# One layer on one core: the opening's weights get two places back in the load queue, and the forget chain runs early on 128 partitions

## The chip, the core and the metric

The kernel runs on one core of one Trainium2 chip. The metric is the device time of one launch, in microseconds (us). Five engines work side by side, each through its own list of instructions in order: TensorE (PE, with weight loads as PEld), VectorE (DVE), ScalarE (ACT), GpSimd (POOL) and SyncE (SP). SP and POOL issue nearly all DMA transfers here; an instruction that waits for a semaphore holds what is behind it on its engine.

## The reference

A decoder layer in float32 for 512 tokens of width 2048: two groups of eight attention heads from one input projection, one output projection, RMSNorm before and after.

```python
h = _rms_norm(x, g_pre)
proj = h @ w_in                      # 2048 x 6472
(q_lat, kv_lat, k_rope_raw, gate_mla,
 fq, fk, fv, f_logit, gate_fox) = jnp.split(proj, split_points, axis=-1)
o_mla = _mla_branch(q_lat, kv_lat, k_rope_raw, ..., cos, sin) * silu(gate_mla)
o_fox = _fox_branch(fq, fk, fv, f_logit, b_forget) * silu(gate_fox)
x = x + _rms_norm(concat([o_mla, o_fox]) @ w_out, g_post)
# in _fox_branch, before its causal softmax attention:
log_f = log_sigmoid(f_logit + b_forget)          # 512 tokens x 8 heads
c = cumsum(log_f, axis=1)
logits = q @ k.T * scale + c[query] - c[key]
# in _mla_branch 64 dimensions of each query and key are turned by the angles
# positions * inv_freq (cos, sin)
```

## The kernel before

Every float32 product is made of three fp32r matmuls: each operand is split into a rounded high part and the rest. For weights, `divide(i)` does this to chunk i: ACT casts `raw` to `whi` (L282), DVE subtracts to get `wlo` (L283). A chunk is mostly 128 partitions x 1024 columns (512 KB); raw, whi and wlo have three buffers each in the pool `wp`. `chunk(i)` asks for the loads of the next chunks and for the splits of the next two. The three matmuls of a term stand at L149, L150 and L151; L150 uses the moving operand's low part or wlo, L151 the other.

The work, in the order of the program:

- *Opening* (`proj_first`). x comes in nine loads (L187, L178: `xa`). For each of 16 blocks k of 128 input columns TensorE transposes the four token tiles (L530), ACT and DVE make `h` (L141, L142), and twelve matmuls (L645) form 328 columns of `w_in`: 256 of the latent, 64 of the rotary key, 8 forget logits. Chunks 0 and 1 hold one block each, chunks 2 to 8 two each. ACT also squares x for the norm (L540). Here ACT, DVE and PE keep the order as written (`manual_schedule`).
- *fq*: chunks 9 to 12, the first pair of FoX queries.
- *v and g* (FoX values and gates): seven products of half size in place of eight, p1, p2, g5, g3, g7, q6, p4, each over four chunks for v and four for g. Chunks 13 to 20 are p1, 21 to 28 p2, 29 to 36 g5, and so on up to chunk 68. The raws of p1 are loaded by `fill` (L235) into tiles `rawv` and `rawg`, five of them in the pool `vr`. When such a chunk is split, POOL adds the next block onto its raw tile by an accumulating DMA (L237). The raws of p2 (L249) take slots of the pool `sp`, which has 28 slots of 4 KB per partition, shared with x, h and most other tiles.
- *Sums of h* for those products (`x_steps`, beside fq and p1): DVE forms `xr` (L1104) and their differences `rmg` (L1003), splits some (L139), and POOL sends each to DRAM (L993, `awaymg`); only when that has landed is its slot free. SP fetches them again later (L1032, `bmg`, `bmq`).
- *Forget chain*. `forget_parts` scales rotary key and logits by the norm's factor (`rft`, tokens on partitions, L781); `rows` transposes that to `rf` (L796, L797), heads on partitions 64 to 71. Then sixteen steps on 8 partitions x 512 columns (tiles `fz`, `fw`, `fd`) form log_sigmoid (L800 to L829) and a scan sums it (L817); SP writes it to `c_dram` (L818). All but `rows` follow the g3 products in the program.
- *Rotary tables*: positions are loaded (L863), 25 DVE steps reduce the angles (L870 to L905), ACT takes three sines (L904 to L907), POOL writes them to DRAM and SP reads them back into `sinT` and `cosT` (L913).
- Then FoX attention, the MLA latents, MLA attention and the output projection. Beside them sums of weight blocks for w_ukv (`t7u` and others) and w_out are made in DRAM, by SP's load and POOL's accumulating DMA (`add_step`, L321, L325).

Outside the opening a scheduler orders each engine's list by its own estimate of when operands are ready; SP's and POOL's transfers can so move far ahead of their place in the program. `in_order` pins an instruction behind the one traced before it on its engine.

Of the kernel before, what the change touches and what calls it, by code (L numbers as in the profile page):

```python
# [12 lines left out]
F32 = mybir.dt.float32  # L13
F32R = mybir.dt.float32r
I32 = mybir.dt.int32
AF = mybir.ActivationFunctionType
ALU = mybir.AluOpType
AX = mybir.AxisListType

P = 128  # L20
D = 2048
S = 512
NT = S // P
NK = D // P
HW = 128
NH = 8
NOPE, ROPE, DV = 128, 64, 128
# [6 lines left out]
O_KR = O_KV + KVR  # L34
# [4 lines left out]
O_F = O_FV + NH * HW  # L39
# [4 lines left out]
L4 = KVR // 2  # L44
KL = L4 + ROPE
# [20 lines left out]
def tile_hybrid_layer(  # L66
# [16 lines left out]
    nc = tc.nc  # L83
    pe, act, dve, pool = nc.tensor, nc.scalar, nc.vector, nc.gpsimd
# [14 lines left out]
    def slot(name, dt=F32, shape=(P, 2, S)):  # L99

        return sp.tile(list(shape), dt, tag="s", name=name)
# [20 lines left out]
    def whole_block(wholes, i, src, scale=None):  # L122
# [5 lines left out]
            act.mul(to, src[:, :P], scale)  # L128
        return to

    def in_order(*instructions):

        for i in instructions:
            tc.keep_in_program_order(i)
# [72 lines left out]
    def add_chunks(w, cols, nk, per, width, first_k=0, single=0):  # L207


        first = len(chunks)  # L210
        k = 0
        while k < nk:
            n = min(1 if k < single else per, nk - k)
            chunks.append((w, cols, first_k + k, n, width))
            k += n
        return range(first, len(chunks))
# [6 lines left out]
    def raw_tile(i):  # L223
        if i in up_chunks:
            return slot(f"raw{i}", shape=(P, 1024))
        pool = more[0] if more and (i - more[1]) % 6 < 3 else wp
        return pool.tile([P, 1024], F32, tag="raw", name=f"raw{i}", bufs=3)

    def fill(i, raw):

        raws[i] = raw
        to = raw.rearrange("p (k c) -> p k c", k=2)
        first, second = chunks[i][0]
        if first is not None:
            in_order(nc.sync.dma_start(to, first))  # L235
        if second is not None:
            pool.dma_start(to, second, accum_op=ALU.add)  # L237

    def load(i, small=None):

        w, cols, k, n, width = chunks[i]
        assert state["step"] >= needs.get(i, -3) + 2
        if cols == "chain":
            return
        if cols is None:

            raw = raw_tile(i)
            for a, b in alike(raw, w):
                nc.sync.dma_start(a, b)  # L249
            raws[i] = raw  # L250
            if k is not None:
                second = slot(f"second{i}")
                nc.sync.dma_start(second, k)
                raws[i] = raw, second.rearrange("p k c -> p (k c)")
            return
        if i < 2:
            raw = slot(f"raw{i}", shape=(P, 1024))
        else:
            raw = raw_tile(i)
        v = raw[:, : n * width].rearrange("p (k c) -> p k c", k=n)  # L260
        for at, off, cnt in cols:
            (nc.sync if cnt >= P or small is None else small).dma_start(
                v[:, :, at : at + cnt],
                w[0, k * P : (k + n) * P, off : off + cnt].rearrange("(k p) c -> p k c", p=P),
            )
        raws[i] = raw

    def join(i):
# [39 lines left out]
    def alike(to, w):  # L308

        if len(w.shape) == 4:  # L310
            to = to.rearrange("p (k h x) -> p k h x", k=2, h=4)
            return [(to[:, k], w[:, k]) for k in range(2)]
        return [(to if len(w.shape) == 2 else to.rearrange("p (k c) -> p k c", k=2), w)]

    def add_step(n, mark):


        if n > 0:
            to, _, second = bg[n - 1]
            for a, b in alike(to, second):  # L320
                pool.dma_start(a, b, accum_op=ALU.add)  # L321
        if 0 <= n < len(bg):
            to, first, _ = bg[n]
            for a, b in alike(to, first):
                nc.sync.dma_start(a, b)  # L325
        if n + 1 < len(bg):
            nc.sync.dma_start(bg[n + 1][0][0:1, 0:16], mark)

# [54 lines left out]
    def plain_in(g, h, c):  # L383
        add_chunks(w_in, [(0, AT[g] + 512 * c, 512)], 8, 2, 512, 8 * h)

    first = add_chunks(w_in, [(0, O_KR - L4, KL), (KL, O_F, NH)], NK, 2, KL + NH, single=2)
    fox = [{} for _ in range(4)]
    chain = {}

# [192 lines left out]
    def wait(n):  # L582
        todo.extend([lambda: None] * n)
# [177 lines left out]
        return g  # L761


    bcol = cst.tile([P, 1], F32, name="bcol")
    pool.memset(bcol, 0.0)
    nc.sync.dma_start(bcol[ROPE : ROPE + NH, :], b_forget.rearrange("o h -> h o"))
    rf = tb.tile([P, S], F32, name="rf")
    pool.memset(rf, 0.0)
    c_dram = dr.tile([NH, S], F32, name="c_dram")
# [2 lines left out]
    def forget_parts(o):  # L772

        r = tmp("rft")
        n = ROPE + NH
        for t in range(NT):
            c = slice(t * n, t * n + NH), slice(t * n + NH, (t + 1) * n)

            for a, b in ((c[0].start, L4), (c[0].start + ROPE, KL)):
                m = ROPE if b < KL else NH  # L780
                dve.tensor_scalar(  # L781
                    out=r[:, a : a + m], in0=o[t][:, b : b + m], scalar1=rcol[:, t : t + 1], scalar2=None,
                    op0=ALU.mult,
                )
        return r

    def forget_sums(r):

        zu, wl, dz = (slot(f"f{i}") for i in "zwd")
        z, u, w, ln, d, zrow = (a[R, i, :] for a in (zu, wl, dz) for i in range(2))  # L790
        n = ROPE + NH

        def rows():
            pt = att_bank("rf")
            for t in range(NT):
                pe.transpose(pt[:n, t * P : (t + 1) * P], r[:, t * n : (t + 1) * n], ident)  # L796
            dve.tensor_copy(rf[:n, :], pt[:n, :])  # L797

        def number(to, src, a, op, b=None, op2=None):
            return lambda: dve.tensor_scalar(  # L800
                out=to, in0=src, scalar1=a, scalar2=b, op0=op, **({"op1": op2} if op2 else {})
            )

        def two(to, x, y, op):
            return lambda: dve.tensor_tensor(out=to, in0=x, in1=y, op=op)

        def both(to, x, a, y, op0, op1):
            return lambda: dve.scalar_tensor_tensor(out=to, in0=x, scalar=a, in1=y, op0=op0, op1=op1)

        def logs():  # L810
            act.activation(ln, w, AF.Ln)

            act.activation(dummy, warm[:, 0:1], AF.Exp)

        def scan():
            pool.memset(zrow, 0.0)
            dve.tensor_tensor_scan(rf[R, :], z, zrow, 0.0, op0=ALU.add, op1=ALU.add)  # L817
            nc.sync.dma_start(c_dram, rf[R, :])  # L818

        return [  # L820
            rows,
            number(z, rf[R, :], bcol[R, :], ALU.add),
            both(u, z, -1.0, z, ALU.mult, ALU.min),
            lambda: act.activation(u, u, AF.Exp),
            number(w, u, 1.0, ALU.add),
            logs,
            number(w, w, -1.0, ALU.add),
            number(d, w, 1e-30, ALU.max),
            lambda: dve.reciprocal(d, d),  # L829
            two(ln, ln, d, ALU.mult),  # L830
            two(ln, ln, u, ALU.mult),
            number(d, w, 0.0, ALU.is_equal),
            two(d, d, u, ALU.mult),
            two(ln, ln, d, ALU.add),
            both(z, z, 0.0, ln, ALU.min, ALU.subtract),
            number(z, z, -1.0, ALU.mult),
            scan,
        ]

    def load_keys(h, wholes):  # L840
        both = slot(f"nk{h}")
# [14 lines left out]

    def rotary_tables():
        ifc = cst.tile([P, 2], F32, name="ifc")
        nc.sync.dma_start(ifc, inv_freq)
        rows = cst.tile([P, 3, P], F32, name="angles")  # L860
        r, n1, n2 = (rows[:, i, :] for i in range(3))
        for b in range(NT):
            nc.sync.dma_start(  # L863
                r[32 * b : 32 * (b + 1), :].bitcast(I32),
                positions[:, b * P : (b + 1) * P].to_broadcast([32, P]),
            )
        steps = []

        def angles():
# [371 lines left out]

    vb = [proj_bank(f"in{t}") for t in range(NT)]
    with tc.manual_schedule(engines={mybir.EngineType.Activation, mybir.EngineType.DVE, mybir.EngineType.PE}):
        proj_first(first, vb)
    make_rcol()
    rft = forget_parts(vb)
    l4 = slot("l4", shape=(P, NT, L4))
# [6 lines left out]
    wait(2)  # L1254
    todo.append(lambda: make_row(rrow, "rrow", *dg))
    set_pace(1000)
    todo.append(fs[0])
    todo.extend([*x_steps(0), *x_steps(1)])
    places = [(g, j) for g in "vg" for j in range(4)]
    for g, j in places[:5]:  # L1260
        fill(prods["p1", g][j], vr.tile([P, 1024], F32, tag="raw", name=f"raw{g}{j}", bufs=5))
# [94 lines left out]
    for g in "vg":  # L1356
# [4 lines left out]
    products(  # L1361
        "vg",
        {
            ("g5", "v"): (1, d3), ("g5", "g"): (1, f7), ("g3", "g", "after"): lambda: todo.extend([*fs[1:], *rotary_tables()]),
            ("g3", "v"): (1, d7), ("g3", "g"): (1, f6), ("g7", "v"): (1, d6),
        },
        out_of,
# [16 lines left out]
    for p in range(4):  # L1384
# [13 lines left out]
            vt = v_slot(3)  # L1398
            later = split_v(3, vt)
        if p == 2:  # L1400
            nc.sync.dma_start(gains[0:6, :], g_q.rearrange("o (k p) -> (o k) p", p=P))
            nc.sync.dma_start(gains[6:10, :], g_kv.rearrange("o (k p) -> (o k) p", p=P))
            make_gcol(gains, NK, 10)
        vs = values_of(f"fv{3 - p}")
        heads = []
# [502 lines left out]
```

## Time and profile before

| What | us |
|---|---|
| Median of 3 runs (lowest, highest) | 914.05 (913.49, 914.98) |
| Profiled execution, its own time | 913.19 |
| Span in its trace | 911.3 |
| PE busy, DVE busy, ACT busy | 881.8, 634.9, 500.7 |
| Mean granted clock | 0.989 |

Busy times are sums over an engine's instructions in the span. "Idle before" stands in brackets in a row, with what ended it. An SPq or POOLq row is the issue of a transfer, and its landing comes later. The rows of a view of stages give the stage's bounds and length, then for PE, PEld, DVE, ACT and POOL the busy time and the number of instructions.

### The profile page before, as it was taken

The page shows a single profiled execution, that of the slowest core. Times are in us where ns is not written, and L with a number is a line of the kernel's source. Part 1 is how long each engine was busy: PE and PEld are TensorE (multiplying, and loading weights), DVE is VectorE, ACT ScalarE, POOL GpSimd, SP SyncE. Part 2 cuts the span into 40 slices and gives each one's busy share as a digit, 9 for nine tenths or more (in the row PEclk, how much of TensorE's full clock was granted, in tenths as well). Part 3 has the DMA queues.
Part 4 walks back from the last instruction along what each step waited for, and adds up shares of the span by engine and source line. Part 5 has one row for each costly group of instructions (what it writes and reads, how often), then busy time and mean ns, then how long its engine had stood idle before and what let it go on. Part 6 is the DMA issues. An engine that isn't in the chain of part 4 may idle for free.

```text
span 911.3 us, 13774 instructions
## 1 busy us (share of the span) xinstructions
PE 881.8 (97%) x5078; PEld 775.2 (85%) x5078; DVE 634.9 (70%) x1056; ACT 500.7 (55%) x915; POOL 125.4 (14%) x133
## 2 busy tenths in 40 slices
PE   9699999989999999999999999999999999999996
PEld 8688899979988888888998999997888888887885
DVE  4589466598555455646655766899797895988786
ACT  6474454445336454444744444557766877645483
POOL 0114103433100010100022344100000000000021
PEclk9799999999999999999999999999999999999999
DMA  9859969989569889884699999568894235789878
GB/s 303 214 167 304 306 200 191 215 160 254 149 144 248 237 216 219 224 202 134 201 285 328 312 225 206 107 198 192 216 212 131 95 116 188 248 315 308 270 223 248
DMA packets 128360, 198.41 MB, mean 218 GB/s; under 512 B 16210, under 2 KB 61164, under 8 KB 127268
## 3 DMA queue, kind: packets, MB, share of 16 engines
q1 hardware_dynamic: 101300, 136.28, 47.8%
q0 software_dynamic: 26256, 61.02, 34.0%
q8 instruction: 40, 0.66, 0.3%
q10 hardware_dynamic: 736, 0.22, 0.1%
q14 instruction: 28, 0.23, 0.1%
HBM read 182.60 MB, written 44.25 MB: 249 GB/s over the span
## 4 chain that ended last, share of the span: by engine, by line
PE 85%; DMA 5%; DVE 5%; ACT 3%; issue 1%; SPq 1%; DVEq 0%; ACTq 0%
PE fq L149 3%; PE fk L151 3%; PE fk L149 3%; PE fk L150 3%; PE fq L151 3%; PE fq L150 3%; PE sm L688 3%; DMA raw<-in_w_in_dram 3%; PE mq L149 2%; PE mq L150 2%; PE mq L151 2%; PE oc L149 2%; PE oa L151 2%; PE oa L150 2%; PE oc L151 2%; PE oc L150 2%
## 5 line engine op out<-in xcount | busy, mean ns | idle before, releaser
L283 DVE TENSOR_TENSOR wlo<-raw,whi 128x1024 fp32r<-128x1024 f32 (+3 forms) x159 | 186.5, 1176 | 117.9 <-ACT whi L282 115.8
L282 ACT CAST whi<-raw 128x1024 fp32r<-128x1024 f32 (+3 forms) x159 | 160.6, 1012 | 160.2 <-PE fk L150 35.4
L149 PE MATMUL fk<-h,whi 128*128 128x512 f32 x128 | 52.5, 410 | 0.0
L149 PE MATMUL fq<-h,whi 128*128 128x512 f32 x128 | 51.0, 399 | 0.0
L151 PE MATMUL fk<-h,wlo 128*128 128x512 f32 x128 | 50.3, 393 | 0.0
L150 PE MATMUL fk<-h,whi 128*128 128x512 f32 x128 | 50.0, 391 | 0.0
L151 PE MATMUL fq<-h,wlo 128*128 128x512 f32 x128 | 50.0, 391 | 0.0
L150 PE MATMUL fq<-h,whi 128*128 128x512 f32 x128 | 50.0, 390 | 0.0
L282 ACT CAST whi<-rawg 128x1024 fp32r<-128x1024 f32 x24 | 25.2, 1051 | 36.2 <-PE vc L151 13.6
L282 ACT CAST whi<-rawv 128x1024 fp32r<-128x1024 f32 x24 | 25.2, 1050 | 34.0 <-PE gg L150 9.2
L282 ACT CAST whi<-rawl 128x1024 fp32r<-128x1024 f32 x25 | 26.2, 1048 | 31.1 <-PE mc L150 7.5
L283 DVE TENSOR_TENSOR wlo<-rawl,whi 128x1024 fp32r<-128x1024 f32 x25 | 30.5, 1223 | 18.0 <-ACT whi L282 18.0
L283 DVE TENSOR_TENSOR wlo<-rawv,whi 128x1024 fp32r<-128x1024 f32 x24 | 29.3, 1223 | 18.1 <-ACT whi L282 18.0
L283 DVE TENSOR_TENSOR wlo<-rawg,whi 128x1024 fp32r<-128x1024 f32 x24 | 29.2, 1222 | 11.2 <-ACT whi L282 11.2
L706 ACT ACTIVATE pf<-pf,stf 128x128 f32<-128x128 f32 (+3 forms) x32 | 18.0, 563 | 31.0 <-DVE stf L697 30.9
L1728 POOL DMA_DIRECT2D c<-in_x_dram x8 | 7.0, 1012 | 202.6 <-ACT c L1727 202.6
L645 PE MATMUL in<-whi,h 128*128 128x328 f32 x128 | 31.4, 333 | 3.4 <-ACT whi L282 3.4
L237 POOL DMA_DIRECT2D rawl<-in_w_in_dram x20 | 23.8, 1192 | 53.5 <-PE ptf L715 31.2
L149 PE MATMUL mq<-ln,whi 128*128 128x512 f32 x72 | 29.0, 403 | 0.0
L151 PEld LDWEIGHTS fq<-h,wlo 128*128 128x128 f32 x128 | 24.0, 188 | 5.3
L151 PEld LDWEIGHTS fk<-h,wlo 128*128 128x128 f32 x128 | 24.0, 188 | 5.3
L151 PE MATMUL mq<-ln,wlo 128*128 128x512 f32 x72 | 28.4, 394 | 0.0
(633 smaller groups left out, 2938.1 us busy)
## 6 DMA issues: line engine op xcount, KB each, us to landing
raw<-in_w_in_dram SPq DMA_DIRECT2D x62, 512.0 KB
raw<-in_w_out_dram SPq DMA_DIRECT2D x32, 512.0 KB
rawl<-in_w_in_dram POOLq DMA_DIRECT2D x20, 512.0 KB, 12.6
rawv<-in_w_in_dram POOLq DMA_DIRECT2D x16, 512.0 KB, 7.2
rawg<-in_w_in_dram POOLq DMA_DIRECT2D x16, 512.0 KB, 9.5
raw<-in_w_in_dram POOLq DMA_DIRECT2D x12, 512.0 KB, 11.9
bmg<-awaymg SPq DMA_DIRECT2D x20, 256.0 KB
rawl<-in_w_in_dram SPq DMA_DIRECT2D x10, 512.0 KB
```

Source lines behind the costliest of these rows:

```text
L149: pe.matmul(o, ah, bh, start=first, stop=False, **kw)
L150: pe.matmul(o, ah, bl, start=False, stop=False, **kw)
L151: pe.matmul(o, al, bh, start=False, stop=last, **kw)
L237: pool.dma_start(to, second, accum_op=ALU.add)
L282: act.copy(hi[:, :m], raw[:, :m])
L283: dve.tensor_tensor(out=lo[:, :m], in0=raw[:, :m], in1=hi[:, :m].bitcast(F32), op=ALU.subtract)
L645: pe.matmul(banks[t][:, :n], a[k][:, tss[t]], b[:, j, :], start=k == 0 and m == 0, stop=k == NK - 1 and m == 2,)
L688: pe.matmul(s[:, :nn], a[:, qs], c[:, :nn], start=(i == 0), stop=(i == len(pairs) - 1))
L706: act.activation(p, p, AF.Exp, bias=st[:, 0:1], scale=unit, accum_out=st[:, 1:2])
L1728: pool.dma_start(to, x[piece(t, c)], accum_op=ALU.add)
```

## The change

There are four parts.

1. *Two places.* `raw_tile` gives chunks 5 and 6 of the opening a tile of the pool `vr`, so they need no buffer that an earlier chunk has to leave.
2. *Nothing ahead.* `queued()` puts SP's transfers behind the load that `load` issued last (`tc.issue_after`: order of issue alone, no wait). It is used for first blocks of `fill`, the sums' loads in `add_step`, the bias, positions and the gains.
3. *Forget chain.* The bias joins in the scaling (one operation on 8 columns per token tile, as many as before). Twelve steps then run on 128 partitions x 32 columns in place, in three groups; `rows` and the scan follow. All of it is put in the program beside fq, and the rotary tables keep their place after g3.
4. Three tiles of 8 x 512 become one (`fz`, zeroed by POOL at the start).

```diff
+    def queued():
+        return tc.issue_after(state["last"])
...
     def raw_tile(i):
+        if i <= opening[-1] and i % 5 < 2:
+            return vr.tile([P, 1024], F32, tag="raw", name=f"raw{i}", bufs=5)
...
         if first is not None:
-            in_order(nc.sync.dma_start(to, first))
+            with queued():
+                nc.sync.dma_start(to, first)
...
+            if small is None:
+                state["last"] = last.ins
...
-    bcol = cst.tile([P, 1], F32, name="bcol")
-    pool.memset(bcol, 0.0)
-    nc.sync.dma_start(bcol[ROPE : ROPE + NH, :], b_forget.rearrange("o h -> h o"))
+    bias = cst.tile([P, NH], F32, name="bias")
+    with queued():
+        nc.sync.dma_start(bias, b_forget.to_broadcast([P, NH]))
...
+            dve.scalar_tensor_tensor(
+                out=r[:, a + ROPE : a + n], in0=o[t][:, KL : KL + NH], scalar=col, in1=bias,
+                op0=ALU.mult, op1=ALU.add,
+            )
...
-        z, u, w, ln, d, zrow = (a[R, i, :] for a in (zu, wl, dz) for i in range(2))
+        z = r[:, : NT * n].rearrange("p (t n) -> p t n", n=n)[:, :, ROPE:]
+        u, w, ln, d = (
+            r[:, NT * n + few * i : NT * n + few * (i + 1)].rearrange("p (t h) -> p t h", h=NH) for i in range(4)
+        )
...
+        return [powers, logs, ends, rows, scan]
...
-    todo.append(fs[0])
-    todo.extend([*x_steps(0), *x_steps(1)])
+    todo.extend(fs[:3])
+    wait(1)
+    todo.extend([*fs[3:], *x_steps(0), *x_steps(1)])
...
-            ... ("g3", "g", "after"): lambda: todo.extend([*fs[1:], *rotary_tables()]),
+            ... ("g3", "g", "after"): lambda: todo.extend(rotary_tables()),
```

The order that comes of it, at three places. In these rows a tile's name is followed by its number in the program (the first chunk's raw is raw0, then a serial number); lines are those of each version's own file, and the new version's stand 6 to 14 further down. First SP's list from the fourth piece of x on, before and then with the change:

```order
L178 DMA xa4_150<-in_x_dram 128x4x256
L178 DMA xa5_155<-in_x_dram 128x4x256
L178 DMA xa6_160<-in_x_dram 128x4x256
L178 DMA xa7_162<-in_x_dram 128x4x256
L766 DMA bcol_167<-in_b_forget_dram 8x1
L235 DMA rawv0_670<-in_w_in_dram 128x2x512
L235 DMA rawv1_672<-in_w_in_dram 128x2x512
L235 DMA rawv2_674<-in_w_in_dram 128x2x512
L235 DMA rawv3_676<-in_w_in_dram 128x2x512
L262 DMA raw5_152<-in_w_in_dram 128x2x320
```

```order
L181 DMA xa4_150<-in_x_dram 128x4x256
L268 DMA raw5_152<-in_w_in_dram 128x2x320
L268 DMA raw5_152<-in_w_in_dram 128x2x8
L181 DMA xa5_155<-in_x_dram 128x4x256
L268 DMA raw6_157<-in_w_in_dram 128x2x320
L268 DMA raw6_157<-in_w_in_dram 128x2x8
L181 DMA xa6_160<-in_x_dram 128x4x256
L181 DMA xa7_162<-in_x_dram 128x4x256
L775 DMA bias_167<-in_b_forget_dram 128x8
L268 DMA raw7_329<-in_w_in_dram 128x2x320
```

Chunks 5 and 6 move between the last pieces of x; chunks 7 to 12 follow, then the fills rawv0 to rawg3, the positions, c_dram and the raws of p2. The new raw12 waits, as before, for the split of raw9 to leave its buffer.

Next DVE's list among the splits of q6's chunks (wlo54 and wlo55 belong to v), before and then with the change; gc and vc are results of g and v.

```order
L283 TENSOR_TENSOR wlo54_1910<-rawv1_672,whi54_1909 128x1024
L829 RECIPROCAL fd_669<-fd_669 8x512
L139 TENSOR_TENSOR bmq63_1713<-bmq63_1713 128x512
L805 TENSOR_TENSOR fw_668<-fw_668,fd_669 8x512
L1296 TENSOR_TENSOR gc2_1508<-gc2_1508,gc0_1814 128x2x256
L805 TENSOR_TENSOR fw_668<-fw_668,fz_667 8x512
L800 TENSOR_SCALAR fd_669<-fw_668 8x512
L1296 TENSOR_TENSOR gc3_1509<-gc3_1509,gc1_1815 128x2x256
L805 TENSOR_TENSOR fd_669<-fd_669,fz_667 8x512
L283 TENSOR_TENSOR wlo55_1945<-rawv2_674,whi55_1944 128x1024
```

```order
L291 TENSOR_TENSOR wlo53_1896<-rawv0_666,whi53_1895 128x1024
L291 TENSOR_TENSOR wlo54_1927<-rawv1_668,whi54_1926 128x1024
L1309 TENSOR_TENSOR gc2_1523<-gc2_1523,gc0_1831 128x2x256
L1309 TENSOR_TENSOR gc3_1524<-gc3_1524,gc1_1832 128x2x256
L291 TENSOR_TENSOR wlo55_1961<-rawv2_670,whi55_1960 128x1024
```

The chain's operations leave this place. Last DVE's list from the split of g's second chunk (18) to p2's first (21), before and then with the change; rmg are sums sent away, xr what they are made of, smg a split of a sum, angles the rotary steps.

```order
L1003 TENSOR_TENSOR rmg32_941<-xr02_876 128x512
L1104 TENSOR_TENSOR xr03_974<-h6_321 128x512
L283 TENSOR_TENSOR wlo18_931<-rawg1_842,whi18_930 128x1024
...
L283 TENSOR_TENSOR wlo20_993<-rawg3_846,whi20_992 128x1024
L139 TENSOR_TENSOR smg53_1043<-rmg53_1041,smg53_1043 128x512
L1003 TENSOR_TENSOR rmg33_1079<-xr13_975,rmg53_1041 128x512
L1003 TENSOR_TENSOR rmg33_1079<-xr03_974 128x512
L283 TENSOR_TENSOR wlo21_1026<-raw21_955,whi21_1025 128x1024
```

```order
L291 TENSOR_TENSOR wlo18_946<-rawg1_848,whi18_945 128x1024
L1015 TENSOR_TENSOR rmg32_956<-xr02_891 128x512
...
L890 TENSOR_SCALAR angles_1733<-angles_1733 128x128
L1015 TENSOR_TENSOR rmg53_1056<-xr03_989,rmg53_1056 128x512
L897 SCALAR_TENSOR_TENSOR angles_1733<-angles_1733 128x128
L1015 TENSOR_TENSOR rmg33_1094<-xr13_990,rmg53_1056 128x512
L291 TENSOR_TENSOR wlo21_1041<-raw21_970,whi21_1040 128x1024
```

The sum rmg32, whose slot rmg33 waits for in both versions (until its transfer away has landed), now stands behind the split of chunk 18, and rotary steps stand among the sums; the chain itself stands further up this list, among wlo12 to wlo14.

More of the change, by code (lines that the diff above doesn't have):

```diff
@@ L261, in load @@
         for at, off, cnt in cols:
-            (nc.sync if cnt >= P or small is None else small).dma_start(
+            last = (nc.sync if cnt >= P or small is None else small).dma_start(
                 v[:, :, at : at + cnt],
@@ L323, in add_step @@
             to, first, _ = bg[n]
-            for a, b in alike(to, first):
-                nc.sync.dma_start(a, b)
+            with queued():
+                for a, b in alike(to, first):
+                    nc.sync.dma_start(a, b)
         if n + 1 < len(bg):
@@ L384, in plain_in @@
         add_chunks(w_in, [(0, AT[g] + 512 * c, 512)], 8, 2, 512, 8 * h)
-    first = add_chunks(w_in, [(0, O_KR - L4, KL), (KL, O_F, NH)], NK, 2, KL + NH, single=2)
+    opening = add_chunks(w_in, [(0, O_KR - L4, KL), (KL, O_F, NH)], NK, 2, KL + NH, single=2)
     fox = [{} for _ in range(4)]
@@ L761, in gate_of @@
         return g
-    bcol = cst.tile([P, 1], F32, name="bcol")
-    pool.memset(bcol, 0.0)
-    nc.sync.dma_start(bcol[ROPE : ROPE + NH, :], b_forget.rearrange("o h -> h o"))
+    bias = cst.tile([P, NH], F32, name="bias")
+    with queued():
+        nc.sync.dma_start(bias, b_forget.to_broadcast([P, NH]))
     rf = tb.tile([P, S], F32, name="rf")
@@ L776, in forget_parts, with number, two, both @@
         for t in range(NT):
[L777 to L784, printed above, removed]
+            a, col = t * n, rcol[:, t : t + 1]
+            dve.tensor_scalar(
+                out=r[:, a : a + ROPE], in0=o[t][:, L4:KL], scalar1=col, scalar2=None, op0=ALU.mult
+            )
[3 more added lines that the diff above has]
+            )
         return r
     def forget_sums(r):
-        zu, wl, dz = (slot(f"f{i}") for i in "zwd")
-        z, u, w, ln, d, zrow = (a[R, i, :] for a in (zu, wl, dz) for i in range(2))
         n = ROPE + NH
+        few = NT * NH
+        z = r[:, : NT * n].rearrange("p (t n) -> p t n", n=n)[:, :, ROPE:]
+        u, w, ln, d = (
+            r[:, NT * n + few * i : NT * n + few * (i + 1)].rearrange("p (t h) -> p t h", h=NH) for i in range(4)
+        )
+        def number(to, src, a, op, b=None, op2=None):
+            dve.tensor_scalar(out=to, in0=src, scalar1=a, scalar2=b, op0=op, **({"op1": op2} if op2 else {}))
+        def two(to, x, y, op):
+            dve.tensor_tensor(out=to, in0=x, in1=y, op=op)
+        def both(to, x, a, y, op0, op1):
+            dve.scalar_tensor_tensor(out=to, in0=x, scalar=a, in1=y, op0=op0, op1=op1)
+        def powers():
+            both(u, z, -1.0, z, ALU.mult, ALU.min)
+            act.activation(u, u, AF.Exp)
+            number(w, u, 1.0, ALU.add)
+        def logs():
+            act.activation(ln, w, AF.Ln)
+            act.activation(dummy, warm[:, 0:1], AF.Exp)
+            number(w, w, -1.0, ALU.add)
+            number(d, w, 1e-30, ALU.max)
+            dve.reciprocal(d, d)
+        def ends():
+            two(ln, ln, d, ALU.mult)
+            two(ln, ln, u, ALU.mult)
+            number(d, w, 0.0, ALU.is_equal)
+            two(d, d, u, ALU.mult)
+            two(ln, ln, d, ALU.add)
+            both(z, z, 0.0, ln, ALU.min, ALU.subtract)
+            number(z, z, -1.0, ALU.mult)
         def rows():
@@ L797, in rows @@
             dve.tensor_copy(rf[:n, :], pt[:n, :])
[L799 to L813, printed above, removed]
-        def scan():
[L816 to L838, printed above, removed]
+        def scan():
+            sums = slot("fz")
+            zeros, total = (sums[R, i, :] for i in range(2))
+            pool.memset(zeros, 0.0)
+            dve.tensor_tensor_scan(total, rf[R, :], zeros, 0.0, op0=ALU.add, op1=ALU.add)
+            nc.sync.dma_start(c_dram, total)
+        return [powers, logs, ends, rows, scan]
     def load_keys(h, wholes):
@@ L858, in rotary_tables @@
         ifc = cst.tile([P, 2], F32, name="ifc")
-        nc.sync.dma_start(ifc, inv_freq)
         rows = cst.tile([P, 3, P], F32, name="angles")
         r, n1, n2 = (rows[:, i, :] for i in range(3))
[L862 to L866, printed above, removed]
+        with queued():
+            nc.sync.dma_start(ifc, inv_freq)
+            for b in range(NT):
+                nc.sync.dma_start(
+                    r[32 * b : 32 * (b + 1), :].bitcast(I32),
+                    positions[:, b * P : (b + 1) * P].to_broadcast([32, P]),
+                )
         steps = []
@@ L1243, in tile_hybrid_layer @@
     with tc.manual_schedule(engines={mybir.EngineType.Activation, mybir.EngineType.DVE, mybir.EngineType.PE}):
-        proj_first(first, vb)
+        proj_first(opening, vb)
     make_rcol()
@@ L1363, in tile_hybrid_layer @@
         {
-            ("g5", "v"): (1, d3), ("g5", "g"): (1, f7), ("g3", "g", "after"): lambda: todo.extend([*fs[1:], *rotary_tables()]),
+            ("g5", "v"): (1, d3), ("g5", "g"): (1, f7), ("g3", "g", "after"): lambda: todo.extend(rotary_tables()),
             ("g3", "v"): (1, d7), ("g3", "g"): (1, f6), ("g7", "v"): (1, d6),
@@ L1400, in tile_hybrid_layer @@
         if p == 2:
-            nc.sync.dma_start(gains[0:6, :], g_q.rearrange("o (k p) -> (o k) p", p=P))
-            nc.sync.dma_start(gains[6:10, :], g_kv.rearrange("o (k p) -> (o k) p", p=P))
+            with queued():
+                nc.sync.dma_start(gains[0:6, :], g_q.rearrange("o (k p) -> (o k) p", p=P))
+                nc.sync.dma_start(gains[6:10, :], g_kv.rearrange("o (k p) -> (o k) p", p=P))
             make_gcol(gains, NK, 10)
```

## The prediction

> **What bounds the kernel now.** I read the page's first lines, then the busy time by stage, then TensorE's own rows where a stage is not full, and last the queues that feed it.
>
> ```profile
> span 911.3 us, 13774 instructions
> PE 881.8 (97%) x5078; PEld 775.2 (85%) x5078; DVE 634.9 (70%) x1056; ACT 500.7 (55%) x915; POOL 125.4 (14%) x133
> ...
> 0.00:25.50 25.50, 23.71 (x161) 22.77 (x161) 9.41 (x15) 15.83 (x46) 2.10 (x12) 1.00 0.96 310
> 25.50:35.00 9.50, 1.33 (x5) 0.74 (x4) 3.65 (x10) 4.51 (x14) 1.38 (x1) 0.62 0.74 207
> 35.00:53.00 18.00, 17.75 (x115) 17.40 (x115) 13.02 (x32) 13.70 (x39) 1.30 (x2) 0.92 0.73 161
> 53.00:75.00 22.00, 22.00 (x101) 18.06 (x101) 21.55 (x45) 10.29 (x19) 5.33 (x7) 1.00 0.77 218
> 75.00:98.00 23.00, 23.00 (x147) 20.98 (x146) 19.14 (x27) 10.86 (x13) 9.48 (x10) 1.00 1.09 291
> 98.00:112.00 14.00, 12.44 (x56) 9.71 (x56) 5.90 (x6) 5.26 (x7) 0.59 (x1) 1.00 1.07 324
> 170.00:300.00 130.00, 126.16 (x692) 109.47 (x691) 87.36 (x128) 60.48 (x91) 27.11 (x26) 0.99 0.86 198
> ```
>
> TensorE is the bound: 881.8 of 911.3 us. In the stage rows the first pair after the length is TensorE, the third VectorE (DVE), the fourth ScalarE (ACT); the last three numbers are granted clock, DMA share, GB/s. Two places leave TensorE idle and are touched by the change: 25.5 to 35 us (1.33 of 9.5 us busy, clock 0.62) and, between 170 and 300 us, 3.84 us. Elsewhere TensorE is full, so a microsecond given back there only returns if it makes TensorE wait.
>
> TensorE's rows and the chain of waits say what the first hole is:
>
> ```profile
> 21.03 0.40 PE L645 MATMUL in<-whi,h 128*128 128x328 f32 x1
> 23.27 0.40 PE L645 MATMUL in<-whi,h 128*128 128x328 f32 x1
> 25.16 0.60 PE L530 MATMUL xt<-ident,xa 128*128 128x128 f32 x4
> 29.12 0.64 PE L645 MATMUL in<-whi,h 128*128 128x328 f32 x1 [3.36 <-ACT whi L282]
> 34.56 0.64 PE L645 MATMUL in<-wlo,h 128*128 128x328 f32 x1 [4.81 <-DVE wlo L283]
> 38.23 0.40 PE L645 MATMUL in<-whi,h 128*128 128x328 f32 x1
> 49.58 0.42 PE L645 MATMUL in<-wlo,h 128*128 128x328 f32 x1 [0.25 <-DVE wlo L283]
> ...
> 14.82 2.62 SPq L235 DMA_DIRECT2D rawv<-in_w_in_dram  x4
> 18.01 1.82 SPq L262 DMA_DIRECT2D raw<-in_w_in_dram  x2
> ...
> 18.01 9.71 DMA raw<-in_w_in_dram
> 28.10 2.88 DMA angles<-in_positions_dram
> 31.17 0.24 DVE angles L870
> ```
>
> Chunk 5 of the opening's weights is issued at 18.01 us behind four fills that only a later product needs, and lands 9.71 us later; its upper half is ready at 29.1. Its lower half then stands on DVE behind the rotary table's first step, which waits for positions that land at 31.0. TensorE stands 3.36 + 4.81 us and restarts at half pace: the last eleven matmuls of that block take from 34.56 to 38.23.
>
> **The change, part by part.** *Opening.* (Old times are this trace's; the new scale is 10.5 us less from 28 us on.) Blocks go at a pitch of 2.24 us (21.03 to 23.27). Without the hole the block that starts at 38.23 starts at 25.16 + 0.35 + 2.24 = 27.75: 10.5 us earlier, the slow restart included. The 0.25 us at 49.58 goes too; the sine tables that delayed ScalarE there move away. I take 10.7. Will the data be there? Up to chunk 5 the queue carries 2.6 MB of x and 1.7 MB of weights; at the 310 GB/s of the first stage it lands near 15 us, against a need near 23. The last piece of x lands near 21 (need 32), chunk 8 near 24 (need 39). Ends: 11 if all goes, 4 if only the rotary steps' half of the hole goes.
>
> What was ahead comes later instead. The eight fills stand behind raw12, which waits for DVE to split raw9; on the new scale this is near 42 us. The first fill is wanted by the row below, on the new scale at 54.5: twelve microseconds for a queue that moves 0.5 MB in under 2. Free, while this cover stands; beyond it every microsecond is one of TensorE.
>
> ```profile
> 64.99 1.06 ACT L282 CAST whi<-rawv 128x1024 fp32r<-128x1024 f32 x1 [0.16 <-PE fq L150]
> ```
>
> *The forget chain where it was.* It stood on 8 partitions by 512 columns among the splits of the last products:
>
> ```profile
> 191.94 3.34 DVE L829 RECIPROCAL fd<-fd 8x512 f32<-8x512 f32 x1
> 207.75 1.22 DVE L817 TENSOR_TENSOR_SCAN rf<-fz,fd 8x512 f32<-8x512 f32 x1
> ...
> 197.59 0.36 PE L149 MATMUL gc<-bmq,whi 128*128 128x256 f32 x1 [1.16 <-DVE gc L1296]
> 199.27 0.38 PE L149 MATMUL gc<-bmq,whi 128*128 128x256 f32 x1 [1.21 <-DVE gc L1296]
> 201.24 0.50 PE L150 MATMUL vc<-wlo,bmq 128*128 128x512 f32 x1 [1.47 <-DVE wlo L283]
> ...
> 183.42 1.28 ACT L824 ACT_TABLE_LOAD   x1 [0.59 <-DVE fz L808]
> 184.72 0.63 ACT L824 ACTIVATE fz<-fz 8x512 f32<-8x512 f32 x1
> ```
>
> The reciprocal alone fills 3.34 us, and TensorE then waits three times for evictions and splits queued behind the chain: 1.16 + 1.21 + 1.47 = 3.84 us, which is all the idle time of the 170 to 300 us stage. With the chain gone DVE has only splits and evictions there; I take all 3.84 (ends 2.4, if the split's wait stays, and 3.84).
>
> *The chain where it goes.* It runs in the 53 to 75 us stage (old times), where DVE is already busy 21.55 of 22 us. Prices:
>
> ```profile
> 54.00 1.39 DVE L781 TENSOR_SCALAR rft<-in,rcol 128x64 f32<-128x64 f32 x8
> 32.81 0.94 DVE L885 SCALAR_TENSOR_TENSOR angles<-angles 128x128 f32<-128x128 f32 x3
> ```
>
> A 128x64 or 128x8 operation takes 0.17 us, a 128x128 one 0.3; twelve on 128x32 lie between, 2.1 to 3.6, with a reciprocal of some 0.35 (3.34 x 32/512 plus a start). The scan keeps its 1.22. I take 3.7 us in all. The bias now joins in the eight scalings, which stay eight: nothing; its 4 KB load is hidden. The transposes that close the chain stand in TensorE's row inside fq, at the time when DVE ends the chain: a wait of about 1 us (0 to 2.5). ScalarE's exp and ln cost two table loads, as before: rows 183.42 and 184.72 show 1.28 us and the work starting 0.02 after. The sum goes by 1.28. [...]
>
> *Who waits for a later DVE.* The splits have a microsecond or two in hand, but the sums sent away by POOL do not:
>
> ```profile
> 85.44 0.59 POOL L993 DMA_DIRECT2D awaymg<-rmg  x1
> awaymg<-rmg POOLq DMA_DIRECT2D x1, 512.0 KB, 11.0
> rawg<-in_w_in_dram POOLq DMA_DIRECT2D x1, 512.0 KB, 14.2
> 96.56 0.69 DVE L1003 TENSOR_TENSOR rmg<-xr,rmg 128x512 f32<-128x512 f32 x1 [3.68 <-DMA awaymg<-rmg]
> 97.77 3.49 DVE L283 TENSOR_TENSOR wlo<-raw,whi 128x1024 fp32r<-128x1024 f32 x3
> 99.05 0.50 PE L150 MATMUL va<-wlo,h 128*128 128x512 f32 x1 [0.36 <-DVE wlo L283]
> 110.45 0.38 PE L149 MATMUL ga<-h,whi 128*128 128x256 f32 x1 [0.44 <-ACT whi L282]
> 111.71 0.39 PE L151 MATMUL ga<-h,wlo 128*128 128x256 f32 x1 [0.76 <-DVE wlo L283]
> ```
>
> DVE's last sum waits for a slot until the transfer issued at 85.44 lands 11.0 us later; the split of chunk 21 is queued behind it, and TensorE already waits 0.36 for that. In the new order this transfer comes after 3.7 us of chain, two table steps (0.5), one more split (1.2) and one more accumulating fill on POOL: issue 4 to 5.3 us later on the old scale. The queue ahead of it is shorter then, since the early transfers leave when they did; I let it land 8.5 to 11 us after issue, so 2 to 4 later than now. One sum instead of two stands before the split, 0.6 back. TensorE waits 1.4 to 3.4 us more; I take 2.3, the transposes' wait included, for whatever TensorE has waited in fq it need not wait here.
>
> *Rotary steps.* 23 of the 25 now lie behind the split of chunk 19, up to that of chunk 26: about six (1.75 us) and a split (1.15) per chunk, 2.9 us where TensorE takes 2.75: 0.2 for each of three chunks, 0.6. The 0.44 + 0.76 at 110 to 112 us go: chunk 25 no longer waits for a transfer away. Net 0.6 gained. The tables' eight loads hold SP until the tables land, with fills behind them that are wanted eight chunks, 22 us, later: nothing.
>
> *The rest.* The sums for w_ukv start after 200 us instead of at 29; about 1.5 MB more fall into a stage with DMA share 0.86, beside products that do not use them yet. Nothing (0 to 1.5).
>
> Sum: 10.7 + 3.84 - 2.3 + 0.6 - 0.2 for the row vector, whose matmuls now come one step earlier = 12.6 us gained. The profiled execution takes 913.19 us (span 911.3 and 1.9 around it); 913.19 - 12.6 = 900.6. The median of the three runs, 914.05, lies 0.86 above it, so I forecast 901.4.
>
> **Rivals.** (1) *DVE hands back most.* The sum that waits for its transfer is hit by the 14.2 us of the slowest fill instead of 8.5 to 11, and the rotary steps cost twice my 0.6: 4 us more is lost, 905 to 908. For it speaks the DMA share of 1.09 in that stage; against it that the tables' loads and rawg fills around it move away. (2) *The opening stays bound by DMA.* Two pieces of weights now stand ahead of the last x. If x arrives as late as the old rate with the old queue would have it, 5 to 7 us of the hole stay: 906 to 908.5. Against it: TensorE had no wait for x after 9 us, and 2 MB less lie ahead. (3) *Slower.* The transfer away that frees DVE's slot lands so late that the split behind it starves TensorE; each microsecond past 98 (old scale) costs one, and it decides at 113, when the 15 us won are used up. That needs 23 us from issue to landing; the longest row is 14.2. It would give 916 or more. (4) *No change:* the early forget chain makes every later fill late by as much as the opening gains, 914. Nothing shows such a coupling: fills are issued when their tiles come free. [...]
>
> **How the numbers follow.** The likeliest case, 897.5 to 904.9, has 0.72: its lower end is all 11 + 3.84 with waits at 110 us gone and only 0.7 lost, its upper end 3.5 us more lost. Rival 1 has 0.13, rival 2 0.06, rival 3 0.04, rival 4 0.03, rival 5, inside the likeliest case's range, 0.02. The range reaches from 897.5 into rivals 1 and 2, to 907.5. By 0.2%, 1.8 us, a measurement of this kernel can tell a change: faster 0.93 (likeliest and rivals 1, 2 and 5), same 0.03, slower 0.04.
>
> **What would show it.** TensorE's rows run through from 4 to some 64 us with no hole at 25 and the opening's last matmul near 42.4, clock 1.0; else rival 2. No wait for gc or vc near 185. The chain's small operations at 0.17 to 0.3 us, in 45 to 60 us. One wait of 2 to 4 us at the first matmuls of chunk 21, near 88, with DVE's sum waiting for the transfer away; if it exceeds 6, rival 1. I am wrong altogether if SP stands at the load of c_dram beyond 80 us or if the fills rawv land after 54.

## The result, and the profile after

The changed kernel takes 900.82 us (median of 4 runs, 899.95 to 901.96) against 913.77 us (the three runs of the table above and a fourth, 912.83 to 914.98): ratio 0.9858, 95% interval 0.9841 to 0.9875. The profiled run takes 899.95 us, 13.24 less than the one before. The forecast was 901.4, but two of its terms were wrong by 2.6 and 3.4 us in opposite directions: that it came so close is luck.

The page's first lines after, and the stages of both kernels, cut at the first matmul of the same products (columns as in the prediction's stage rows). Before, then after: opening, fq, p2, q6.

```profile
span 898.2 us, 13763 instructions
PE 877.7 (98%) x5078; PEld 773.3 (86%) x5078; DVE 624.6 (70%) x1055; ACT 499.1 (56%) x914; POOL 125.2 (14%) x132
```

```profile
0.00:53.10 53.10, 42.89 (x277) 41.01 (x278) 26.19 (x56) 34.14 (x99) 4.78 (x14) 0.90 0.84 241
53.10:75.90 22.80, 22.80 (x104) 18.71 (x103) 22.25 (x45) 10.19 (x19) 5.90 (x8) 1.00 0.79 227
98.29:123.09 24.80, 23.24 (x147) 20.51 (x145) 11.55 (x10) 10.33 (x13) 1.91 (x3) 1.00 0.92 284
190.35:219.24 28.89, 25.05 (x146) 21.79 (x145) 26.50 (x31) 9.63 (x12) 11.33 (x11) 0.94 0.90 189
```

```profile
0.00:41.74 41.74, 40.38 (x277) 39.39 (x278) 20.55 (x34) 33.02 (x97) 2.58 (x12) 1.00 0.67 204
41.74:65.42 23.68, 22.93 (x104) 18.70 (x103) 22.76 (x54) 10.90 (x20) 4.91 (x6) 1.00 0.94 295
87.81:117.04 29.23, 24.07 (x147) 21.57 (x145) 18.77 (x33) 12.84 (x17) 2.55 (x4) 0.94 0.94 271
184.30:206.72 22.42, 22.42 (x147) 20.53 (x145) 15.03 (x19) 9.63 (x12) 11.12 (x11) 1.00 1.11 232
```

The lengths give the ledger: opening 53.10 - 41.74 = 11.36 won, fq 0.88 lost, p2 4.43 lost, q6 6.47 won. p1 and the products from g5 to g7 take the same in both (22.39 and 67.26 us); all that comes behind q6, up to the last 9 us, wins 0.48. The sum is 13.00, of the 13.10 by which the spans differ.

A product like p2 or q6 takes 22.42 us with TensorE full, as q6 does now. So p2 lost 2.38 us before and loses 6.81 now. TensorE's rows after show where, with DVE's and POOL's rows that made it:

```profile
58.60 0.60 PE L839 MATMUL rf<-ident,rft 128*72 128x128 f32 x4 [0.75 <-DVE rft L806]
93.37 0.79 PE L153 MATMUL va<-wlo,h 128*128 128x512 f32 x1 [5.16 <-DVE wlo L291]
93.96 0.63 PE L154 MATMUL va<-whi,h 128*128 128x512 f32 x1
98.05 0.39 PE L152 MATMUL va<-whi,h 128*128 128x512 f32 x1
...
77.66 1.05 POOL L1005 DMA_DIRECT2D awaymg<-rmg  x1
91.49 0.69 DVE L1015 TENSOR_TENSOR rmg<-xr,rmg 128x512 f32<-128x512 f32 x1 [7.88 <-DMA awaymg<-rmg]
92.09 1.22 DVE L291 TENSOR_TENSOR wlo<-raw,whi 128x1024 fp32r<-128x1024 f32 x1
```

DVE's sum starts 13.8 us after the transfer's issue at 77.66, having stood 7.88 us for it with chunk 21's split behind. TensorE idles 5.16 us, the only idle time of the stage, and then runs its next matmuls at 0.63 instead of 0.39 us; that is the other 1.65 of the 6.81.

### The profile page after: what moved, and what is told of

Its sections match the earlier page's. It is cut to its first block, busy times and chain, and to the rows that moved or that the text cites. A ratio compares the mean times of both kernels' runs of the same rounds, so it can differ in the third digit from the quotient of the medians.

```text
span 898.2 us, 13763 instructions
## 1 busy us (share of the span) xinstructions
PE 877.7 (98%) x5078; PEld 773.3 (86%) x5078; DVE 624.6 (70%) x1055; ACT 499.1 (56%) x914; POOL 125.2 (14%) x132
## 4 chain that ended last, share of the span: by engine, by line
PE 79%; DMA 9%; DVE 6%; ACT 3%; issue 2%; POOL 1%; SPq 0%; DVEq 0%; POOLq 0%; ACTq 0%
DMA raw<-in_w_in_dram 5%; PE fk L152 3%; PE fk L154 3%; PE fk L153 3%; PE in L654 3%; PE fq L152 3%; PE fq L153 3%; PE sm L697 3%; PE fq L154 3%; DVE wlo L291 2%; PE mq L152 2%; PE mq L153 2%; PE mq L154 2%; PE sf L697 2%; PE oa L154 2%
## 6 DMA issues: line engine op xcount, KB each, us to landing
raw<-in_w_in_dram POOLq DMA_DIRECT2D x12, 512.0 KB, 11.2
```

## The experiments

**The two halves alone.** *Opening alone* keeps the old forget chain in its old place; *chain alone* keeps the old loads.

```diff
 # opening alone, against the change
-    todo.extend(fs[:3]); wait(1); todo.extend([*fs[3:], *x_steps(0), *x_steps(1)])
+    todo.append(fs[0]); todo.extend([*x_steps(0), *x_steps(1)])      # old forget_parts, forget_sums
-    ("g3", "g", "after"): lambda: todo.extend(rotary_tables()),
+    ("g3", "g", "after"): lambda: todo.extend([*fs[1:], *rotary_tables()]),
 # chain alone: the kernel before with the opposite lines; no queued(), no two places
```

> The opening's two places and the queue alone; the forget chain stays on 8 x 512 in the place it had before. Theory (the gains add up and the handed-back wait at chunk 21 is half the chain's work on DVE, half a slower transfer): the opening gives 11.4 us, the 6.5 us around q6 stay lost, the wait at chunk 21 shrinks from 5.2 to 2 to 3 us: 904 to 906. Rival A (that wait is made by the DMA work the opening moves together, the chain has no part in it): it stays at 5 us, 907 to 908. Rival B (it is the chain's alone): it goes, 902 to 903.

> The forget chain early on 128 x 32, the opening's loads as before. Theory: 6.5 us won around q6 (3.84 of waits and 2.6 of half-rate matmuls behind them), 0.9 lost at the transposes, 1.5 to 2.7 more wait at chunk 21: 909.5 to 911. Rival A (that wait comes of DMA work alone): no more wait there, 908 to 908.5. Rival C (around q6 only the 3.84 us of waits are won): 912 to 913.

Measured: opening alone 902.95 us (900.19 to 904.34), ratio 0.9881 [0.9854, 0.9908]; chain alone 911.42 (910.74 to 913.53), 0.9978 [0.9966, 0.9990]. The p2 and q6 stages, of opening alone and then of chain alone, with the transfer's issue and TensorE's wait:

```profile
89.27:114.65 25.38, 23.57 (x147) 20.29 (x145) 18.12 (x34) 12.93 (x17) 2.63 (x4) 1.00 1.06 311
181.91:211.28 29.37, 25.84 (x147) 22.34 (x146) 26.49 (x31) 9.62 (x12) 11.35 (x11) 0.88 0.91 194
...
78.59 1.06 POOL L1004 DMA_DIRECT2D awaymg<-rmg  x1
88.62 0.69 DVE L1014 TENSOR_TENSOR rmg<-xr,rmg 128x512 f32<-128x512 f32 x1 [2.68 <-DMA awaymg<-rmg]
91.24 0.50 PE L153 MATMUL va<-wlo,h 128*128 128x512 f32 x1 [1.58 <-DVE wlo L291]
```

```profile
99.34:127.73 28.39, 24.29 (x146) 21.61 (x145) 12.14 (x11) 10.44 (x13) 1.99 (x3) 0.94 0.95 290
194.99:217.41 22.42, 22.42 (x146) 20.53 (x145) 15.03 (x19) 9.63 (x12) 11.08 (x11) 1.00 1.11 234
...
89.78 0.59 POOL L994 DMA_DIRECT2D awaymg<-rmg  x1
104.09 0.69 DVE L1004 TENSOR_TENSOR rmg<-xr,rmg 128x512 f32<-128x512 f32 x1 [6.87 <-DMA awaymg<-rmg]
106.58 0.80 PE L150 MATMUL va<-wlo,h 128*128 128x512 f32 x1 [4.10 <-DVE wlo L283]
```

The opening alone lengthens p2 by 0.58 us (24.80 to 25.38), the chain alone by 3.59 (to 28.39). The hand-back at chunk 21 is the chain's, nearly all of it: the opening alone came out in rival B's range and not in the theory's, which gave the opening half, and rival A fell in both runs. Without the wait's share the chain is worth its 6.47 us at q6 (rival C is out, 22.42 against 28.89); with it, 2.7, and the time lies 0.4 above the theory's range. The chain's place and its shape were changed together: no run keeps the 128 x 32 chain in its old place, so what the shape alone would bring at q6 stays open.

The transfer leaves 12.85 us ahead of p2's first product before, 10.68 with the opening alone, 9.56 with the chain alone, 10.15 with both. It takes 11.1, 10.0, 14.3 and 13.8 us until the waiting sum starts. So the chain alone costs twice: the issue comes 3.3 us later and the transfer takes 3.2 us longer. Beside the opening, which makes the issue 2.2 us later by itself, the chain adds 0.5 and 3.8. Why the transfer takes longer stays open.

**The opening, taken apart.** Places without the queue, the queue without places, and the change with the positions alone let out of the queue.

```diff
 # places only
 def queued():
-    return tc.issue_after(state["last"])
+    return nullcontext()
 # queue only
-        if i <= opening[-1] and i % 5 < 2:
-            return vr.tile([P, 1024], F32, tag="raw", name=f"raw{i}", bufs=5)
 # positions ahead, in rotary_tables
-        with queued():
-            nc.sync.dma_start(ifc, inv_freq); ...
+        nc.sync.dma_start(ifc, inv_freq); ...
```

> All of the change but the queue: the fills, the positions and the sums may be issued where the scheduler likes. Chunks 5 and 6 still stand ahead of them in SP's list. Theory: the two places alone close the hole, since they let chunks 5 and 6 stand between the last pieces of x; fills then use the DMA time that is idle from 25 to 42 us, the transfer that chunk 21 waits for lands earlier, and the wait there falls to 1 to 3 us: 896 to 899. Rival D (the queue closes the hole; positions and fills ahead of chunk 7 make it wait, and the rotary steps hold DVE in the opening): 4 to 6 us of hole come back, 903 to 906.

> All of the change but the two places: chunks 5 and 6 take buffers that chunks 2 and 3 have to leave, and stand behind the last piece of x in SP's list. Theory: chunk 5 then lands near 21 to 24 us against a need near 23, so 0 to 2 us of hole: 900.5 to 903. Rival D' (the places are needed): chunk 5 lands beyond 25 and the hole is 3 us or more with a half-rate restart: 904 to 907.

> The change with the positions alone (18 KB with inv_freq) free to be issued early; the fills and sums stay behind. In DVE's list the first rotary step then stands behind the split of chunk 2, ahead of block 3. Theory: these small loads are issued behind the last piece of x and land at 21 to 24 us; DVE stands there from some 11 us on, TensorE idles 6 to 9 us and restarts at half rate: 906 to 911. Rival H (what delayed the positions before were the 2 MB of fills ahead of them; without these they are there in time): no hole, rotary steps done by 30 us, the wait at chunk 21 half a us shorter: 899 to 901.

Measured: places only 913.28 us (911.79 to 916.13), 0.9997 [0.9984, 1.0011]; queue only 901.51 (900.19 to 902.24), 0.9868 [0.9846, 0.9890]; positions ahead 914.95 (913.49 to 917.01), 1.0018 [1.0005, 1.0030]. Rows of places only, then of positions ahead, then the start of fq in queue only:

```profile
29.46 0.23 DVE L882 CAST angles<-angles 128x128 f32<-128x128 int32 x1 [13.17 <-DMA angles<-in_positions_dram]
30.40 0.92 PE L654 MATMUL in<-whi,h 128*128 128x328 f32 x2 [11.16 <-DVE h L145]
```

```profile
18.18 2.50 SPq L874 DMA_DIRECT2D angles<-in_positions_dram  x4
24.10 0.23 DVE L881 CAST angles<-angles 128x128 f32<-128x128 int32 x1 [12.25 <-DMA angles<-in_positions_dram]
25.89 1.46 PE L654 MATMUL in<-whi,h 128*128 128x328 f32 x4 [11.23 <-DVE h L145]
```

```profile
42.77 0.39 PE L152 MATMUL fq<-h,whi 128*128 128x512 f32 x1
```

The queue brings the opening's gain: without it the places win nothing (the theory had 896 to 899), and without the places all of the gain stays but 1 us at most. fq then starts at 42.77 and not 41.74, but the seven other kernels here with both parts start it between 41.73 and 42.38, and the times of 901.51 and 900.82 are not separate. The positions are enough to lose it: these 65 KB (four loads of 16 KB and one of 1, not the 18 of the expectation) are issued from 17.70 on behind the last of x, land near 24, and DVE has stood since 11.8 with the next `h` queued behind its first rotary step. That costs 14.1 us against the change, more than the 5 to 10 that the theory gave: it had taken a wait of 6 to 9 us where 11.23 came. Whether the fills ahead would lose it too, without the positions, no run shows. Rival D was right in the loss (the times are worse still than its 903 to 906), rivals H and D' fell.

**The wait at chunk 21.** Five fills are issued behind chunk 9's load; or the last two sums stand behind the products of g; or the rotary steps stay at their place in the program.

```diff
 # fills in idle time, for the first five fills (state["early"]: chunk 9's load)
-            with queued():
+            with tc.issue_after(state["early"]):
 # sum behind split, in away_steps and ahead of p2
+        if (of, j) == ("m", 3):
+            behind.extend(steps[2:]); steps = steps[:2]
     drain()
+    wait(0)
+    todo.extend(behind)
 # rotary late
-            dve.tensor_copy(n1, r.bitcast(I32))
+            in_order(dve.tensor_copy(n1, r.bitcast(I32)))
```

> The change with five of the eight fills issued right behind chunk 9's load, into the time from 25 to 42 us in which the DMA moves some 20 GB/s. Theory: 2.5 MB less in the stages that follow, the transfer that chunk 21 waits for lands in 10 to 11 us and not 13.8, the wait falls from 5.2 to 2 or 3.5 us: 897 to 899.5. Rival E (its length is set by what stands around it at 72 to 92 us, which does not change): wait and time as with the change, 900 to 902.

> The change with the last two sums of the fourth block (the two that wait for the slot) put in the program behind the products of g, so that on DVE the splits of chunks 21 to 23 stand ahead of them. Theory: the late transfer costs nothing but the place of these sums in DVE's order; the 5.2 us and the half-rate matmuls behind them go: 894 to 896. Rival F (slots stay short: another wait for a transfer comes in DVE's or SP's list at chunks 22 to 28 and gives 3 us or more back): 897.5 to 900.

> The change with the rotary steps pinned at their place behind the g3 products, so that none stands among DVE's splits of chunks 17 to 26; the sum still stands ahead of chunk 21's split. Theory: the steps cost little themselves (some 0.5 us of the transfer's later issue), the wait at chunk 21 stays at 4 to 5.2 us: 899.5 to 901. Rival I (the rotary steps, not the chain, bring the wait): it falls below 2 us, 896 to 898.

Measured: fills 900.05 us (896.33 to 900.30), 0.9841 [0.9815, 0.9867]; sum behind split 894.74 (894.23 to 896.42), 0.9796 [0.9776, 0.9816]; rotary late 901.04 (900.24 to 902.56), 0.9857 [0.9840, 0.9875]. Rows of the fills, of the sum behind the split, and of rotary late:

```profile
91.46 0.50 PE L153 MATMUL va<-wlo,h 128*128 128x512 f32 x1 [3.21 <-DVE wlo L293]
91.80 0.40 PE L154 MATMUL va<-whi,h 128*128 128x512 f32 x1
```

```profile
78.17 1.05 POOL L1006 DMA_DIRECT2D awaymg<-rmg  x1
88.33:112.69 24.36, 23.34 (x147) 20.47 (x146) 14.59 (x26) 12.84 (x17) 2.55 (x4) 1.00 0.95 293
94.96 0.50 PE L153 MATMUL va<-wlo,h 128*128 128x512 f32 x1 [0.77 <-DVE wlo L291]
95.02 0.68 DVE L1016 TENSOR_TENSOR rmg<-xr,rmg 128x512 f32<-128x512 f32 x1
```

```profile
93.73 0.79 PE L153 MATMUL va<-wlo,h 128*128 128x512 f32 x1 [4.87 <-DVE wlo L291]
```

Moving the last two sums, of which the waiting one had stood ahead of chunk 21's split, behind three splits takes p2 from 29.23 to 24.36 us and the program to 894.74: the transfer is issued as late as before, the sum no longer waits when its turn comes at 95.02, and rival F fell. This version beats both kernels. The rotary steps are not the cause (rival I fell). The earlier fills leave a wait of 3.21 us in the profiled run, and no slow restart behind it; that run is also the fastest of the four by 3.7 us. The other three took 900.0 to 900.3, within rival E's range, so whether the fills help is not settled. (The DMA moved 68 GB/s from 25 to 42 us in the changed kernel, not the 20 of the expectation.)

**Does idling cost more than its time?** Twenty matmuls whose result nobody reads, ahead of chunk 21's first product.

```diff
+    hot = att_bank("hot")
+    for i in range(20):
+        in_order(pe.matmul(hot, hh[0][:, :P], hh[0], start=True, stop=True))
     for g in "vg":
         one("p2", g, ...)
```

> The change with twenty further 128 x 512 matmuls on TensorE, whose result nobody reads, right ahead of chunk 21's first product, where TensorE idles 5.2 us. Theory (the matmuls at 0.63 us behind the wait are due to the idling): the clock stays at 1.00 there, the rows behind the wait read 0.39 us, and 1.2 to 1.4 us are won although work is added: 899 to 900.2. Rival G (the half rate has another cause, such as the DMA load): the same slow rows, 900.5 to 902.

> The kernel e9_rotary_late with the twenty further matmuls ahead of chunk 21's first product; DVE's, ScalarE's and the DMA queues' orders are the same in both. Theory (the half rate behind a wait comes of the idling): TensorE's rows behind the wait read 0.39 us, and the program is 1.2 to 1.4 us shorter than e9_rotary_late. Rival G (added work is only added): equal or longer.

The first one took 903.87 us (903.65 to 904.28), 0.9894 [0.9873, 0.9915]: 3 us longer than the change, and outside what either side had expected. Its rows:

```profile
93.21 0.50 PE L153 MATMUL va<-wlo,h 128*128 128x512 f32 x1 [0.39 <-DVE wlo L291]
93.55 0.40 PE L154 MATMUL va<-whi,h 128*128 128x512 f32 x1
...
102.17 0.31 ACT L916 ACTIVATE angles<-angles 128x128 f32<-128x128 f32 x1 [6.75 <-DVE angles L914]
103.88 0.50 PE L152 MATMUL va<-whi,h 128*128 128x512 f32 x1 [2.41 <-ACT whi L290]
```

The slow restart is gone (0.40 us at once), but the scheduler, presumably because it counted the added matmuls as time, put the rotary sines ahead of chunk 24's cast on ScalarE, where they waited 6.75 us for DVE; TensorE lost 2.41 there. So the pair was run again with the rotary steps late in both, which leaves the other engines' orders equal. With the matmuls: 898.46 us (897.22 to 899.61), 0.9827 [0.9810, 0.9844], against 901.04 without. The p2 stage (the added matmuls included) and its stretch from 94 to 97 us, without and with them:

```profile
88.46:118.07 29.61, 24.74 (x147) 22.01 (x145) 13.28 (x12) 10.95 (x13) 2.01 (x3) 0.88 0.83 251
94.00:97.00 3.00, 3.00 (x8) 2.33 (x9) 2.55 (x3) 0.64 (x2) 0.56 (x1) 0.50 1.07 300
```

```profile
88.03:115.90 27.87, 27.25 (x167) 24.21 (x165) 13.28 (x12) 10.96 (x13) 2.01 (x3) 1.00 0.88 270
94.00:97.00 3.00, 3.00 (x15) 2.47 (x14) 2.42 (x3) 1.09 (x3) 0.56 (x1) 1.00 1.10 323
```

With twenty matmuls more the stage is 1.74 us shorter, and 15 matmuls fit where 8 did, at about the same DMA share (1.10 and 1.07). Rival G fell: the half rate came with 4.87 us of idling and not with the 0.62 us that the twenty matmuls left of it. The program is 2.6 us shorter by the medians, more than the 1.2 to 1.4 forecast. Of the 2.6 us between the two spans 0.4 lies ahead of fq, where the two programs are the same, and 0.4 behind the stage is not explained.

**Everything together**, with the chain's transposes behind the first sums (`[*x_steps(0), *fs[3:], *x_steps(1)]`):

> Everything together: the change with the last sums behind the splits, five fills in the idle DMA time, the rotary steps late, and the chain's transposes put behind the first sums of h. Theory: against e6_sum_behind_split's 894.7 the waits at 59 (0.75 us and 0.1 behind it), 95 (0.77) and 104 us (0.26) go: 892.5 to 894. Rival J (those short waits only hid others): 894.5 to 896.

Measured 894.38 us (892.91 to 894.77), 0.9778 [0.9759, 0.9797], not to be told from the 894.74 with only the sums moved. The wait at the transposes is gone; waits of 0.32 and 0.77 us at p2 stay. The time lies between the theory's 892.5 to 894 and rival J's 894.5 to 896, and settles neither.

```profile
94.20 0.50 PE L153 MATMUL va<-wlo,h 128*128 128x512 f32 x1 [0.77 <-DVE wlo L293]
```

## Why the prediction was right, and where it was wrong

| Term | forecast | measured |
|---|---|---|
| Opening | 10.7 | 11.36 |
| Row vector and transposes in fq, p2, rotary steps | -0.2 - 2.3 + 0.6 | -0.88 - 4.43 |
| Forget chain leaves q6 | 3.84 | 6.47 |
| Behind q6 | 0 | 0.48 |
| Sum | 12.64 | 13.00 |

The mechanisms were for the most part those forecast; the sizes at q6 and at p2 were not. That the sums differ by only 0.36 us is luck: q6 gave 2.6 us more than forecast, and fq and p2 took 3.4 us more.

*Opening: right in size, half wrong in cause.* The hole is gone and the opening's last matmul starts at 41.59 (42.4 forecast). Chunk 5 behind the fills and the rotary step ahead of a split were taken as two halves, "4 if only the rotary steps' half goes". They don't add up: with chunk 5 early and the positions free the hole is 11.2 us, longer than both halves. Rival 2 did not come: TensorE's only wait for x is 0.23 us. The first fill was there when ScalarE cast it at 53.26, and SP issued the write to c_dram at 62.12, so the two signs of being wrong altogether are absent.

*The forget chain at q6: mis-sized by 2.6 us.* The step took "all 3.84", the waits in brackets, as all the loss. The stage lost 28.89 - 22.42 = 6.47. The rows of before behind the third wait show the rest:

```profile
201.81 0.58 PE L150 MATMUL vc<-wlo,bmq 128*128 128x512 f32 x1
202.61 0.63 PE L149 MATMUL vc<-whi,bmq 128*128 128x512 f32 x1
203.04 0.63 PE L150 MATMUL vc<-wlo,bmq 128*128 128x512 f32 x1
205.46 0.40 PE L150 MATMUL vc<-wlo,bmq 128*128 128x512 f32 x1
```

Nine matmuls take the 3.65 us from 201.81 to 205.46, up to 0.43 us each and not 0.23: 1.6 us. The last 1.0 I put down to the three breaks in the matmuls' overlap (in the stream they take 0.39 us each, 0.23 apart), an estimate that no run took apart. The prediction had counted such a restart in the opening and forgotten it here. Behind a single gap of 3.21 us (the earlier fills) the matmuls went on at full pace, behind 4.10 (chain alone) and 5.16 they did not, and the half pace lasted 3.1 us (the change, from 93.37) to 4.4 (rotary late, from 93.73). At q6 no single gap exceeded 1.47 us, but three made 3.84 us idle within 5, and the clock read 0.50 from 202 to 205 us.

*Handed back: mis-sized by 3.4 us the other way.* The mechanism was the one forecast (chunk 21's split behind a sum that waits for the transfer away). The step that failed is "I let it land 8.5 to 11 us after issue": it took 13.8, and the half-rate matmuls behind a 5.16 us wait were left out once more. The issue itself came less late than forecast, 2.7 us on the old scale where 4 to 5.3 were taken, and the two waits of 0.44 and 0.76 us at 110 to 112 us went as forecast. Rival 1 had the transfer right (14.2 us) and so named the place and the size (5.16, short of its 6), but not the q6 term that paid for it. The rotary steps, priced at 0.2 for each of three chunks, cost nothing in p2 that a run could tell. The row vector's matmuls, priced at 0.2, show no wait. Rivals 3 and 4 (slower, no change) are out by the time alone.

*The chain's price was right*: its twelve steps take 0.17 to 0.34 us each, 2.35 in all, and the scan 1.22: 3.57 where 3.7 was taken. The transposes waited 0.75 us (1 taken). The table loads, from ScalarE's rows after:

```profile
48.75 1.28 ACT L816 ACT_TABLE_LOAD   x1
50.05 0.23 ACT L816 ACTIVATE rft<-rft 128x32 f32<-128x32 f32 x1
50.29 1.28 ACT L820 ACT_TABLE_LOAD   x1
51.59 0.23 ACT L820 ACTIVATE rft<-rft 128x32 f32<-128x32 f32 x1
```

Each takes 1.28 us and the work starts 0.02 us behind it. No run shows a dearer switch of tables, for which rival 5 has its 0.02.

*The range's lower end* does not come out of its own terms: 11 + 3.84 with the 1.2 us of waits gone and 0.7 lost gives 15.3 us and 898.7, not 897.5.

## What to carry to other kernels

Price a stall of TensorE by the length of its stage against the same work at full pace, not by the idle time in brackets (at q6 6.47 us, not 3.84). In a list that runs in order, look for the operation that waits for a transfer and what stands behind it: moving the waiting sum behind three splits won 6 us by the medians, though its transfer left as late as before. Issue order mattered by what waited for the data, not by size: 65 KB of positions that the next `h` stood behind on DVE cost 14.1 us.

## What was not expected of the hardware

- Work added shortened a program: twenty useless matmuls (4.6 us of TensorE) made it 2.6 us faster by the medians, 1.74 in the stage itself, because the clock stayed at 1.00 from 94 to 97 us, where it was 0.50 without them.
- 65 KB of loads in the wrong place of one queue cost 14.1 us, more than the whole change brings.
- The same 512 KB transfer away took 10.0 to 14.3 us from its issue to the start of the sum that waits for it, with DMA shares that hardly differ where both were read (1.10 over the 11.1 us before, 1.09 over the 13.8 us after); what sets it stays open.
- Three gaps of 1.16 to 1.47 us close to each other (q6 before) were followed by the half pace, clock 0.50; one gap of 3.21 us in another run (the earlier fills) was not.
